# Rotary queries turned in PSUM by transposed tables and spread per head by one matmul

## The chip, the cores and the metric

The kernel runs on one core of a Trainium2 chip. The metric is the device time of one launch in microseconds. The core's engines are TensorE (PE in the profile, its weight loads PEld), VectorE (DVE), ScalarE (ACT), GpSimd (POOL) and SyncE (SP), which issues the DMAs. Each engine works through its own queue in order and waits on semaphores.

## The reference

A decoder trunk of two layers over 1024 tokens of width 1024, in f32. Each layer feeds four causal mixers in parallel, gates and merges them, and ends in a layer norm. The change lies in the first mixer (MLA), in the queries' rotary part:

```python
q = (_rms_norm(c_q, q_norm) @ w_qb).reshape(b, s, MLA_HEADS, MLA_NOPE + MLA_ROPE)   # 4 heads, 64 + 32
q_nope, q_pe = q[..., :MLA_NOPE], q[..., MLA_NOPE:]
q_pe = _rope(q_pe, cos[:, :, None, :], sin[:, :, None, :])
...
def _rope(x, cos, sin):
    x1, x2 = jnp.split(x, 2, axis=-1)
    return jnp.concatenate([x1 * cos - x2 * sin, x1 * sin + x2 * cos], axis=-1)
```

`cos` and `sin` depend on the token's position and on 16 frequencies only; they are the same for all heads and both layers. The scores are `concat(q_nope, q_pe) . concat(k_nope, k_pe)`, scaled by 96 ** -0.5.

## The kernel before

**Precision.** An f32 product is made of three fast matmuls (fp32r): each operand is split into a high part and a rest (`wh`, `wl`; `cqh`, `cql`), and high x high, low x high and high x low are added in PSUM. These are the three lines of `passes` (L255 to L257). For attention operands a helper, `stack_pair`, takes a PSUM tile with two heads of 64 channels on 128 partitions and makes two tiles, `opA` for the first head and `opB` for the second: ACT writes the rounded 64 rows (`lead`), DVE the remainder in the other 64 partitions (`rest`). In its default order it runs lead a, rest a, lead b, rest b; with `copies_first` both leads run first.

**PSUM.** There are eight banks in three pools: four for projections (`PJ`; pj, pb, pg, qpeT and so on take them in turn), two for transposes (`PT`; pt, vtp, qpe, rqb, qpT) and two for the attention output (`PY`). A tile takes a bank when the last reader of the tile before has finished.

**Order.** The program is written with generators: `run(units, filler, total)` walks the attention units and, in the gaps between their matmuls, steps a filler (the next branch's projections) so that `total` steps are spread evenly. Around the MLA queries, `main` is such a chain, and between its steps the merge of another branch is stepped (`mg`: rows pb, the branch product, pg, the merge gate, ACT's sigmoid mg and DVE's acc). The final order on each engine follows from it and from the waits.

**The stage of the MLA queries,** once per layer. `load_wq` splits three tiles of `w_qb` on POOL. `split_cq(half)` scales and splits the compressed queries of 512 tokens (row norm spread by the transposes rqb, L993). `mla_q` makes the 64 plain channels of the four heads by two pj groups of nine matmuls. `mla_qpe` makes the 4 x 32 rotary channels: nine matmuls into qpeT (channels on partitions), an ACT copy (L1028), four transposes to tokens on partitions (L1032), six DVE steps of rope (L721 to L726), a scaling on POOL (L1038), and ACT and DVE make the high part and the rest side by side (L1044, L1045), each twice over. `mla_qpT` turns these back per head, four transposes each (L1053), and ACT casts the result to `qpe` (L1055): 128 partitions that hold high, rest, high, rest of 32 channels, which the score matmul (L386) multiplies with the key's rotary part. Half 1 comes before half 0, and `mla_qpT(1)` and part of `(0)` run beside the first attention unit.

**The forgetting stage** (fox) of layer 0 is the first attention of the kernel: two runs of eight units, the first with the projections of the second pair as its filler. The values are transposed there too (vtp), and p by PT tiles (pt). `cosT` and `sinT` (128 tokens x 8 blocks x 16 frequencies) are computed by then.

Of the kernel before, what the change touches and what calls it, by code (L numbers as in the profile page):

```python
# [66 lines left out]
def decoder_trunk(ctx: ExitStack, tc: tile.TileContext, x, x_t, mem_t, positions, w_a, w_s, mla_q_norm, mla_w_qb,  # L67
# [19 lines left out]
    def nm(s):  # L87
        uid[0] += 1
        return f"{s}_{uid[0]}"
# [107 lines left out]
    c_d = dp.tile([4, S], F32, name="c_d")  # L197

# [448 lines left out]

    for layer in range(DEPTH):
# [229 lines left out]
        run(fox_units(fox[0], 0), pair_qkv(fox[1], SC64), 49)  # L878
# [126 lines left out]
        def load_wq():  # L1005
            for k in range(3):
                raw = rp.tile([P, HALF], F32, tag="wr", name=nm("wr"))
                nc.sync.dma_start(raw[:, :384], mla_w_qb[layer, k * P:(k + 1) * P, :])
                h, l = U("wqh"), U("wql")
                sv = raw[:, :384].rearrange("p (h c) -> p h c", h=4)  # L1010
                for c0, c1, d0 in ((0, 64, 0), (64, 96, 256)):
                    n = 4 * (c1 - c0)
                    hv, lv = (t[:, d0:d0 + n].rearrange("p (h c) -> p h c", h=4) for t in (h, l))
                    split_pool(sv[:, :, c0:c1], hv, lv)
                wq_h.append(h)
                wq_l.append(l)
# [6 lines left out]

        def mla_qpe(half):
            ps = PJ("qpeT")
            yield from passes(ps, wsl(wq_h, wq_l, 3, 256), cqT[half], 3)
            qT = U("qT", F32)
            act.copy(qT, ps)  # L1028
            yield QPE_STEPS
            ps = PT("qpe")  # L1030
            for b in range(4):
                pe.transpose(ps[:, b * P:(b + 1) * P], qT[:, b * P:(b + 1) * P], ident)  # L1032
            src = ps.rearrange("p (b h c) -> p b h c", b=4, h=4)
            qr = U("qr", F32).rearrange("p (b h c) -> p b h c", b=4, h=4)
            qt = TMP("qt")[:, :256].rearrange("p (b h c) -> p b h c", b=4, h=4)
            cs, sn = (t[:, 4 * half:4 * half + 4].unsqueeze(2).broadcast_to((P, 4, 4, 16)) for t in (cosT, sinT))
            rope(qr, src, cs, sn, qt, dve.tensor_tensor)
            pool.tensor_scalar(qr, qr, SC96, 1.0, ALU.mult, ALU.mult)  # L1038
            for b2 in range(2):
                t4 = wp.tile([P, 2, 4, 4, ROPE], F32R, tag="W", name=nm("qt4"))  # L1040
                for b in range(2):
                    t = t4[:, b]
                    qb_ = qr[:, 2 * b2 + b].unsqueeze(2).broadcast_to((P, 4, 2, ROPE))
                    act.copy(t[:, :, 0::2, :], qb_)  # L1044
                    dve.tensor_tensor(t[:, :, 1::2, :], qb_, f(t[:, :, 0::2, :]), ALU.subtract)  # L1045
                    t4s[half].append(t)
            yield

        def mla_qpT(half):
            for h in range(4):  # L1050
                pt = PT("qpT")
                for b in range(4):
                    pe.transpose(pt[:, b * P:(b + 1) * P].bitcast(F32R), t4s[half][b][:, h].rearrange("p a c -> p (a c)"), ident_r)  # L1053
                o = U("qpe")
                act.copy(o, pt)  # L1055
                qpe[h][half] = o
                yield
            t4s[half].clear()
# [89 lines left out]
        def step(f):  # L1148
# [3 lines left out]
        main = chain(mla_ckvT(), mla_k(0), mla_k(1), step(load_wq), step(lambda: load_cq(1)), mla_v(0), mla_v(1),  # L1152
                     split_cq(1), step(lambda: load_cq(0)), mla_qpe(1), split_cq(0), mla_q(1), mla_qpe(0), mla_qpT(1), mla_q(0), mla_qpT(0))
# [172 lines left out]
```

## Time and profile before

| | |
|---|---|
| time, median of 3 runs | 1568.74 us (1568.33 to 1569.33) |
| time of the profiled execution | 1568.4 us |
| its span on the core | 1566.7 us |
| PE busy | 1551.5 us, 99% |
| DVE busy | 1032.2 us, 66% |
| ACT busy | 724.0 us, 46% |
| POOL busy | 778.3 us, 50% |
| mean granted TensorE clock | 0.999 |

Busy rows of PE overlap one another, since a matmul starts before the one ahead has drained; the distance between two starts tells what one costs. In the groups of instructions the columns are: line, engine, operation, output and inputs, partitions x elements, count, then busy time, mean duration in ns, and the idle time in front with what ended it. In the timeline they are: start, length, engine, line, operation. In the windows: the stretch, its length, busy time of PE, PEld, DVE, ACT and POOL with the number of instructions, the granted clock, the DMA share and the GB/s.

### The profile page before, as it was taken

The page shows a single profiled execution, that of the slowest core. Times are in us where ns is not written, and L with a number is a line of the kernel's source. Part 1 is how long each engine was busy: PE and PEld are TensorE (multiplying, and loading weights), DVE is VectorE, ACT ScalarE, POOL GpSimd, SP SyncE. Part 2 cuts the span into 40 slices and gives each one's busy share as a digit, 9 for nine tenths or more (in the row PEclk, how much of TensorE's full clock was granted, in tenths as well). Part 3 has the DMA queues.
Part 4 walks back from the last instruction along what each step waited for, and adds up shares of the span by engine and source line. Part 5 has one row for each costly group of instructions (what it writes and reads, how often), then busy time and mean ns, then how long its engine had stood idle before and what let it go on. Part 6 is the DMA issues. An engine that isn't in the chain of part 4 may idle for free.

```text
span 1566.7 us, 24759 instructions
## 1 busy us (share of the span) xinstructions
PE 1551.5 (99%) x8446; PEld 1326.5 (85%) x8446; DVE 1032.2 (66%) x2055; ACT 724.0 (46%) x1608; POOL 778.3 (50%) x951
## 2 busy tenths in 40 slices
PE   9999999999999999999999999999999999999997
PEld 8888888888888888888898888888888888888886
DVE  7455687755436788872853566887554367888738
ACT  5355565545434656440323556655354346564300
POOL 5666536555544334671336655365565443346600
PEclk9999999999999999999999999999999999999999
DMA  6421112132233221252313211121322332212413
GB/s 186 115 71 42 46 47 71 58 95 82 74 110 109 73 65 31 81 175 74 125 62 101 58 51 45 41 75 51 108 70 80 103 112 73 63 37 83 154 53 115
DMA packets 86062, 127.92 MB, mean 82 GB/s; under 512 B 13425, under 2 KB 38833, under 8 KB 85937
## 3 DMA queue, kind: packets, MB, share of 16 engines
q1 hardware_dynamic: 85936, 126.34, 26.5%
q8 instruction: 67, 1.10, 0.3%
q14 instruction: 59, 0.48, 0.1%
HBM read 89.57 MB, written 19.96 MB: 70 GB/s over the span
## 4 chain that ended last, share of the span: by engine, by line
PE 97%; DVE 1%; ACT 1%; DMA 0%; issue 0%; SPq 0%; POOL 0%; DVEq 0%; ACTq 0%
PE pj L255 13%; PE pj L257 13%; PE pj L256 13%; PE y L502 8%; PE pt L472 7%; PE pb L255 4%; PE pb L256 4%; PE pb L257 4%; PE po L257 4%; PE po L256 4%; PE po L255 4%; PE sc L384 4%; PE sc L383 4%; PE pg L255 2%; PE pg L256 2%; PE pg L257 2%
## 5 line engine op out<-in xcount | busy, mean ns | idle before, releaser
L255 PE MATMUL pj<-xTh,wh 128*128 128x512 f32 x832 | 334.4, 402 | 2.3 <-DVE mx L441 1.4
L257 PE MATMUL pj<-xTh,wl 128*128 128x512 f32 x832 | 327.4, 394 | 0.0
L256 PE MATMUL pj<-xTl,wh 128*128 128x512 f32 x832 | 326.3, 392 | 0.0
L167 POOL TENSOR_TENSOR wl<-wr,wh 128x512 fp32r<-128x512 f32 x168 | 224.2, 1336 | 10.1
L156 DVE TENSOR_TENSOR pl<-pt,ph 128x384 fp32r<-128x384 f32 (+1 forms) x272 | 171.3, 638 | 84.9 <-ACT ph L155 82.8
L164 POOL TENSOR_SCALAR wh<-wr 128x512 fp32r<-128x512 f32 x168 | 113.0, 673 | 216.7 <-PE pj L256 145.6
L155 ACT CAST ph<-pt 128x384 fp32r<-128x384 f32 (+1 forms) x272 | 147.6, 549 | 156.1 <-PE pt L472 151.3
L257 PEld LDWEIGHTS pj<-xTh,wl 128*128 128x128 f32 x832 | 156.3, 188 | 31.5
L453 POOL TENSOR_SCALAR p<-p,sm 128x896 f32<-128x896 f32 (+7 forms) x128 | 101.1, 792 | 158.6 <-DVE sm L452 153.6
L255 PEld LDWEIGHTS pj<-xTh,wh 128*128 128x128 f32 x832 | 156.7, 188 | 25.1 <-DVE mx L441 1.8
L256 PEld LDWEIGHTS pj<-xTl,wh 128*128 128x128 f32 x832 | 156.7, 188 | 22.6
L135 ACT ACTIVATE p<-p,mx 128x896 f32<-128x896 f32 (+7 forms) x128 | 99.5, 777 | 72.7 <-DVE mx L441 63.6
L502 PE MATMUL y<-pl,v 128*128 128x256 f32 (+1 forms) x544 | 122.3, 302 | 0.0
L135 ACT ACTIVATE mg<-pg 128x512 f32<-128x512 f32 x128 | 76.0, 597 | 80.5 <-PE pg L257 38.6
L472 PE MATMUL pt<-ident_r,p 128*128 128x128 f32 x704 | 111.2, 273 | 0.2
L502 PE MATMUL y<-ph,v 128*128 128x256 f32 (+1 forms) x544 | 111.1, 280 | 0.0
L446 DVE TENSOR_TENSOR_SCAN kt<-kt,unseen 128x896 f32<-128x896 f32 (+3 forms) x64 | 96.0, 1502 | 20.2 <-ACT kt L135 19.7
L502 PEld LDWEIGHTS y<-ph,v 128*128 128x128 f32 x544 | 94.7, 189 | 13.5
L255 PE MATMUL pb<-ybh,wh 128*128 128x512 f32 x256 | 103.0, 402 | 0.4
L256 PE MATMUL pb<-ybl,wh 128*128 128x512 f32 x256 | 100.2, 391 | 0.0
L257 PE MATMUL pb<-ybh,wl 128*128 128x512 f32 x256 | 100.0, 391 | 0.0
L472 PEld LDWEIGHTS pt<-ident_r,p 128*128 128x128 f32 x704 | 85.7, 140 | 15.1 <-issue 0.5
(272 smaller groups left out, 3551.1 us busy)
## 6 DMA issues: line engine op xcount, KB each, us to landing
wr<-in_w_s_dram SPq DMA_DIRECT2D x168, 256.0 KB, 2.7
s<-opA SPq DMA_DIRECT2D x128, 64.0 KB, 2.0
s<-opB SPq DMA_DIRECT2D x128, 64.0 KB, 2.0
wr<-in_w_out_dram SPq DMA_DIRECT2D x32, 256.0 KB, 2.6
xr<-in_x_t_dram SPq DMA_DIRECT2D x16, 256.0 KB, 4.8
ckb<-c_d SPq DMA_DIRECT2D x8, 512.0 KB, 4.0
y_d<-y SPq DMA_DIRECT2D x16, 256.0 KB, 2.1
y<-y_d SPq DMA_DIRECT2D x16, 256.0 KB, 3.9
```

The source lines that it names most:

```text
L135: i = act.activation(*args, **kw)
L155: act.copy(h, src)
L156: return dve.tensor_tensor(l, src, f(h), ALU.subtract)
L164: i = pool.tensor_scalar(h, src, 1.0, 1.0, ALU.mult, ALU.mult)
L167: pool.tensor_tensor(l, src, f(h), ALU.subtract)
L255: pe.matmul(ps, ah, bh, start=k == 0, stop=False)
L256: pe.matmul(ps, ah, bl, start=False, stop=False)
L257: pe.matmul(ps, al, bh, start=False, stop=k == nk - 1)
L446: dve.tensor_tensor_scan(kt[:, ::-1], kt[:, ::-1], unseen[:, S - w:][:, ::-1], 1.0, ALU.mult, ALU.max)
L453: pool.tensor_scalar(p, p, sm, 1.0, ALU.mult, ALU.mult)
L472: pe.transpose(pt[:, c:c + P], self.p[i][:, b * P:(b + 1) * P], ident)
L502: pe.matmul(u.y[:, q0 * P:256], u.op["v"][b][:, u.head, :], src[:, s * 256 + q0 * P:s * 256 + 256], start=j == 0 and n == 0, stop=j == n_c ...
```

## The change

The rotation is done where the projection has left its result, in PSUM with channels on partitions. For that the tables must lie with channels on partitions too: `rotary_tables`, a generator stepped once in layer 0 behind the filler of the first fox run (`total` 53 in place of 49), spreads cosine and sine over the heads on POOL (`rows`), transposes them by blocks (`tab`), scales them on ACT (the sine with its sign per 32 rows) and stores them (`tab_d`). Each layer loads them by halves. In `mla_qpe` four DVE multiplications of 32 partitions take the swapped halves times sine from PSUM, one multiplies the PSUM tile by cosine in place, one adds in place. For this the weight columns are laid out so that the 128 channels are, for each of two pairs of heads, first half of both, second half of both. `stack_pair` then makes two stacked tiles, and in `mla_qpT` one matmul per head with a selection matrix (`pick`, copied from the identity) spreads them to the layout that `qpe` had.

```diff
+    def rotary_tables():
+        for n, src in enumerate((cosT, sinT)):
+            for half in range(2):
+                rows = U("rows", F32)
+                pool.tensor_scalar(rows.rearrange("p (b r c) -> p b r c", b=4, r=8),
+                                   src[:, 4 * half:4 * half + 4, :].unsqueeze(2).broadcast_to((P, 4, 8, 16)), 1.0, 1.0, ALU.mult, ALU.mult)
+                ps = PT("tab")
+                for b in range(4):
+                    pe.transpose(ps[:, b * P:(b + 1) * P], rows[:, b * P:(b + 1) * P], ident)
+                t = TMP("tab")
+                if n == 0:
+                    act.activation(t, ps, AF.Copy, scale=SC96)
+                else:
+                    for r0 in range(0, P, 32):
+                        act.activation(t[r0:r0 + 32, :], ps[r0:r0 + 32, :], AF.Copy, scale=-SC96 if r0 % 64 else SC96)
+                nc.sync.dma_start(tab_d[half][:, n, :], t)
+                yield
...
-        run(fox_units(fox[0], 0), pair_qkv(fox[1], SC64), 49)
+        tables = () if layer else rotary_tables()
+        run(fox_units(fox[0], 0), chain(pair_qkv(fox[1], SC64), tables), 49 if layer else 53)
...
+        def load_tabs(half):
+            tabs[half] = K("tab").rearrange("p (a n) -> p a n", a=2)
+            nc.sync.dma_start(tabs[half], tab_d[half])
+            if not pick:
+                pick.append(U("pick")[:, :2 * P].rearrange("p (e r q c) -> p e r q c", e=2, r=2, q=4))
+                for e in range(2):
+                    for r in range(2):
+                        act.copy(pick[0][:, e, r], ident.rearrange("p (q e c) -> p e q c", q=4, e=2)[:, e])
+
         def mla_qpe(half):
             ps = PJ("qpeT")
             yield from passes(ps, wsl(wq_h, wq_l, 3, 256), cqT[half], 3)
-            qT = U("qT", F32)
-            act.copy(qT, ps)
+            tab = tabs.pop(half)
+            t = U("qt", F32)
+            for r0 in range(0, P, 32):
+                r1 = r0 + 32 if r0 % 64 == 0 else r0 - 32
+                dve.tensor_tensor(t[r0:r0 + 32, :], ps[r1:r1 + 32, :], tab[r1:r1 + 32, 1], ALU.mult)
+            dve.tensor_tensor(ps, ps, tab[:, 0], ALU.mult)
+            dve.tensor_tensor(ps, ps, t, ALU.add)
             yield QPE_STEPS
-            ps = PT("qpe")
...
+            d = [[None, None], [None, None]]
+            stack_pair(d, 1.0)(ps, half)
+            t4s[half] += [d[0][half], d[1][half]]
             yield
 
         def mla_qpT(half):
             for h in range(4):
                 pt = PT("qpT")
-                for b in range(4):
-                    pe.transpose(pt[:, b * P:(b + 1) * P].bitcast(F32R), t4s[half][b][:, h].rearrange("p a c -> p (a c)"), ident_r)
+                pe.matmul(pt, pick[0][:, h % 2].rearrange("p r q c -> p (r q c)"), t4s[half][h // 2], start=True, stop=True)
```

In `main`, `load_tabs(1)` follows `load_cq(1)` and `load_tabs(0)` follows `load_cq(0)`. In `load_wq` the rotary columns of a weight tile are split in two pieces of 64 columns (one per pair of heads) where one piece of 128 stood.

Three places show how the order moves. First TensorE behind the last matmuls of half 1's qpeT in layer 0. Before, a pb and a pg group are followed by the transposes of qpe and rqb and then by the first pj group of `mla_q(1)`:

```order
L255 MATMUL pb_5990<-ybh_5394,wh_5749 128x512
L256 MATMUL pb_5990<-ybl_5395,wh_5749 128x512
L257 MATMUL pb_5990<-ybh_5394,wl_5750 128x512
L255 MATMUL pg_6009<-mrh_3836,wh_5749 128x512
L256 MATMUL pg_6009<-mrl_3837,wh_5749 128x512
L257 MATMUL pg_6009<-mrh_3836,wl_5750 128x512
L1032 MATMUL qpe_5925<-ident_r,qT_5902 128x128 x4
L993 MATMUL rqb_5949<-ident_r,rq_643 128x128 x4
L255 MATMUL pj_5999<-cqh_5836,wqh_5643 128x512
```

After, between the two pj groups of `mla_q(1)` on the same engine (the first ends here, the second begins), a pg group and the first two spreading matmuls:

```order
L256 MATMUL pj_6048<-cqh_5927,wqh_5710 128x512
L257 MATMUL pj_6048<-cql_5928,wqh_5710 128x512
L258 MATMUL pj_6048<-cqh_5927,wql_5711 128x512
L256 MATMUL pg_6111<-mrh_3790,wh_5806 128x512
L257 MATMUL pg_6111<-mrl_3791,wh_5806 128x512
L258 MATMUL pg_6111<-mrh_3790,wl_5807 128x512
L1081 MATMUL qpT_6154<-opA_5992,pick_5732 128x512
L1081 MATMUL qpT_6158<-opA_5992,pick_5732 128x512
L256 MATMUL pj_6070<-cqh_5896,wqh_5690 128x512
```

The transposes of qpe are gone, and both groups of rqb stand together far ahead; the first qpeT_5945 has 24 matmuls from its own last to this pj_6070, which takes its bank, and pj_6048 takes the bank of pb_5977. Second, DVE at the same place. Before, the rotation (qr, qt), the row norm of the compressed queries (cq) and acc alternate:

```order
L721 TENSOR_TENSOR qr_5930<-qpe_5925,cosT 128x16x16
L722 TENSOR_TENSOR qt_5931<-qpe_5925,sinT 128x256
L724 TENSOR_TENSOR qr_5930<-qpe_5925,sinT 128x16x16
L995 TENSOR_TENSOR cq_5877<-cq_5877,rqb_5949 128x512
L995 TENSOR_TENSOR cq_5879<-cq_5879,rqb_5949 128x512
L995 TENSOR_TENSOR cq_5881<-cq_5881,rqb_5949 128x512
L723 TENSOR_TENSOR qr_5930<-qr_5930,qt_5931 128x16x16
```

After:

```order
L1017 TENSOR_TENSOR cq_5941<-cq_5941,rqb_5998 128x512
L1069 TENSOR_TENSOR qt_5964<-qpeT_5945,tab_5730 32x512 x4
L1133 SCALAR_TENSOR_TENSOR acc_5984<-mg_5975,pb_5977 128x512
L1070 TENSOR_TENSOR qpeT_5945<-qpeT_5945,tab_5730 128x512
L1071 TENSOR_TENSOR qpeT_5945<-qpeT_5945,qt_5964 128x512
L313 SCALAR_TENSOR_TENSOR opA_5992<-qpeT_5945,opA_5992 64x512
L313 SCALAR_TENSOR_TENSOR opB_5993<-qpeT_5945,opB_5993 64x512
```

The quarter multiplications now stand ahead of the acc that reads pb_5977, and all of the rotation and stacking reads the PSUM tile qpeT_5945. Third, TensorE in layer 0's first fox run, where after the change the cosine's two tab groups stand around a score pair ahead of a projection group:

```order
L258 MATMUL pj_1681<-xTh_212,wl_1422 128x512
L659 MATMUL tab_1603<-ident_r,rows_1601 128x128 x4
L384 MATMUL sc_1798<-opA_1295,opA_1041 128x256
L385 MATMUL sc_1798<-opA_1295,s_349_1652 128x256
L659 MATMUL tab_1613<-ident_r,rows_1611 128x128 x4
L256 MATMUL pj_1807<-xTh_397,wh_1415 128x512
```

Before, the projection groups run on between the same kind of rows (s is the query with its halves swapped, loaded by SP):

```order
L257 MATMUL pj_1634<-xTh_203,wl_1455 128x512
L383 MATMUL sc_1734<-opA_1321,opA_1049 128x128
L384 MATMUL sc_1734<-opA_1321,s_337_1605 128x128
L255 MATMUL pj_1634<-xTh_211,wh_1454 128x512
L256 MATMUL pj_1634<-xTl_212,wh_1454 128x512
```

The sine's two groups follow 20 rows later, side by side, and the next transposes of p (pt) some 30 rows behind them.

More of the change, by code (lines that the diff above doesn't have):

```diff
@@ L197, in decoder_trunk @@
     c_d = dp.tile([4, S], F32, name="c_d")
+    tab_d = dp.tile([2, P, 2, HALF], F32, name="tab_d")
     def rsqrt(dst, m, n):
@@ L1010, in load_wq @@
                 sv = raw[:, :384].rearrange("p (h c) -> p h c", h=4)
[L1011 to L1014, printed above, removed]
+                hv, lv = (t[:, :256].rearrange("p (h c) -> p h c", h=4) for t in (h, l))
+                split_pool(sv[:, :, 0:64], hv, lv)
+                for g in range(2):
+                    d0 = 256 + 64 * g
+                    hv, lv = (t[:, d0:d0 + 64].rearrange("p (t e c) -> p t e c", t=2, e=2) for t in (h, l))
+                    split_pool(sv[:, 2 * g:2 * g + 2, 64:96].rearrange("p e (t c) -> p t e c", t=2), hv, lv)
                 wq_h.append(h)
@@ L1022, in mla_q @@
                 stack_pair(ml[pair]["q"], SC96, True)(ps, half)
+        tabs = {}
+        pick = []
+        def load_tabs(half):
[6 more added lines that the diff above has]
+                        act.copy(pick[0][:, e, r], ident.rearrange("p (q e c) -> p e q c", q=4, e=2)[:, e])
         def mla_qpe(half):
@@ L1026, in mla_qpe @@
             yield from passes(ps, wsl(wq_h, wq_l, 3, 256), cqT[half], 3)
-            qT = U("qT", F32)
-            act.copy(qT, ps)
-            yield QPE_STEPS
-            ps = PT("qpe")
-            for b in range(4):
[L1032 to L1046, printed above, removed]
+            tab = tabs.pop(half)
[5 more added lines that the diff above has]
+            dve.tensor_tensor(ps, ps, t, ALU.add)
+            yield QPE_STEPS
+            d = [[None, None], [None, None]]
+            stack_pair(d, 1.0)(ps, half)
+            t4s[half] += [d[0][half], d[1][half]]
             yield
@@ L1051, in mla_qpT @@
                 pt = PT("qpT")
-                for b in range(4):
-                    pe.transpose(pt[:, b * P:(b + 1) * P].bitcast(F32R), t4s[half][b][:, h].rearrange("p a c -> p (a c)"), ident_r)
+                pe.matmul(pt, pick[0][:, h % 2].rearrange("p r q c -> p (r q c)"), t4s[half][h // 2], start=True, stop=True)
                 o = U("qpe")
@@ L1150, in step @@
             yield
-        main = chain(mla_ckvT(), mla_k(0), mla_k(1), step(load_wq), step(lambda: load_cq(1)), mla_v(0), mla_v(1),
-                     split_cq(1), step(lambda: load_cq(0)), mla_qpe(1), split_cq(0), mla_q(1), mla_qpe(0), mla_qpT(1), mla_q(0), mla_qpT(0))
+        main = chain(mla_ckvT(), mla_k(0), mla_k(1), step(load_wq), step(lambda: load_cq(1)), step(lambda: load_tabs(1)), mla_v(0), mla_v(1),
+                     split_cq(1), step(lambda: load_cq(0)), step(lambda: load_tabs(0)), mla_qpe(1), split_cq(0), mla_q(1), mla_qpe(0), mla_qpT(1), mla_q(0), mla_qpT(0))
         def early():
```

## The prediction

> **What bounds the kernel.** I read the page from the top (busy time, then the chain that ended last), then the windows around the two places that the change touches, then the timeline there.
>
> ```profile
> span 1566.7 us, 24759 instructions
> ...
> PE 1551.5 (99%) x8446; PEld 1326.5 (85%) x8446; DVE 1032.2 (66%) x2055; ACT 724.0 (46%) x1608; POOL 778.3 (50%) x951
> ...
> PE 97%; DVE 1%; ACT 1%; DMA 0%; issue 0%; SPq 0%; POOL 0%; DVEq 0%; ACTq 0%
> ```
>
> TensorE is the path: 97% of the chain. Work taken from another engine is worth something only where TensorE waits for it, and a new wait of TensorE costs its full length.
>
> ```profile
> 75.00:160.00 85.00, 84.19 (x475) 72.20 (x475) 51.53 (x145) 46.14 (x102) 54.55 (x82) 1.00 0.22 60
> 485.00:532.00 47.00, 46.13 (x236) 37.90 (x235) 32.41 (x72) 26.23 (x53) 12.73 (x14) 1.00 0.21 60
> 1265.00:1312.00 47.00, 46.15 (x237) 37.92 (x236) 32.35 (x72) 26.17 (x53) 12.75 (x14) 1.00 0.20 60
> ```
>
> The first column after the length is PE, then PEld, DVE, ACT and POOL. The first window lies in layer 0's forgetting-attention stage, where the tables will be built; the others are the MLA query stage of the two layers. All are full on PE, and the two layers are alike, so I cost one MLA stage and double it. The clock is 1.00.
>
> A busy TensorE row overlaps the next, so I price matmuls by the distance between starts:
>
> ```profile
> 495.09 0.39 PE L256 MATMUL qpeT<-cql,wqh 128*128 128x512 f32 x1
> 495.31 0.39 PE L257 MATMUL qpeT<-cqh,wql 128*128 128x512 f32 x1
> ...
> 500.31 0.60 PE L1032 MATMUL qpe<-ident_r,qT 128*128 128x128 f32 x4
> 500.75 0.60 PE L993 MATMUL rqb<-ident_r,rq 128*128 128x128 f32 x4
> 501.10 0.48 PE L255 MATMUL pj<-cqh,wqh 128*128 128x512 f32 x1
> 501.42 0.39 PE L256 MATMUL pj<-cql,wqh 128*128 128x512 f32 x1
> ...
> 505.07 0.39 PE L257 MATMUL pj<-cqh,wql 128*128 128x512 f32 x1
> 505.56 0.47 PE L255 MATMUL qpeT<-cqh,wqh 128*128 128x512 f32 x1
> ...
> 513.85 0.60 PE L1032 MATMUL qpe<-ident_r,qT 128*128 128x128 f32 x4
> 514.20 0.30 PE L1053 MATMUL qpT<-ident_r,qt 128*128 128x128 f32 x1
> 514.34 0.45 PE L255 MATMUL pj<-cqh,wqh 128*128 128x512 f32 x1
> 514.62 0.39 PE L256 MATMUL pj<-cql,wqh 128*128 128x512 f32 x1
> ...
> 519.96 0.40 PE L257 MATMUL pj<-cqh,wql 128*128 128x512 f32 x1
> 520.20 0.79 PE L1053 MATMUL qpT<-ident_r,qt 128*128 128x128 f32 x8
> 520.82 0.47 PE L383 MATMUL sc<-opA,opA 128*128 128x512 f32 x1
> 521.13 0.40 PE L384 MATMUL sc<-opA,s 128*128 128x512 f32 x1
> ...
> 524.72 0.40 PE L257 MATMUL pg<-mrh,wl 128*128 128x512 f32 x1
> 525.68 0.53 PE L1053 MATMUL qpT<-ident_r,qt 128*128 128x128 f32 x4 [0.57 <-ACT qpe L1055]
> ...
> 527.67 0.50 PE L255 MATMUL pb<-ybh,wh 128*128 128x512 f32 x1
> ```
>
> A 512-column matmul takes 0.227 us (495.09 to 495.31; 505.07 would have been followed at 505.30). Four f32 transposes take 0.35 (500.75 to 501.10, 0.088 each), a short one 0.078 (8 from 520.20 to 520.82). The matmul behind a group of transposes starts its follower about 0.08 late (501.10 to 501.42 is 0.32), which I call the switch.
>
> **What goes on TensorE, per layer.** The two groups at L1032 go: 0.44 (500.31 to 500.75) and 0.35 (513.85 to 514.20), and one switch of 0.09, as the two rqb groups now stand side by side: -0.88. Head 0's four transposes, which lie singly between pj matmuls from 514.20 on, go: 4 x 0.078 and three switches of 0.06 (514.34 to 514.62 is 0.28): -0.49. The two spreading matmuls that take their place outside the start of attention: 2 x 0.227 = +0.45. The gap of 0.26 at 505.07 ends when qpeT of half 0 finds its operands; it now comes a pair of pj groups later, so it goes: -0.26.
>
> The start of attention, 519.96 to 527.67, holds the other 28 transposes. By count they cost 28 x 0.078 and five switches, 2.58; six matmuls cost 1.36, so 1.2 us could go. But this stretch waits: for ACT's casts of qpT (0.57 at 525.68) and for DVE's row maxima, and the casts stay, eight of them, behind the same leads of the new query tiles. Walking the new order with these durations, the same wait for a cast grows from 0.7 to 1.0 and the stretch ends at 7.0 to 7.2 us in place of 7.71: -0.6, half of the count.
>
> **What comes, per layer: a bank held by a chain.** Before, one ACT copy (L1028) freed the qpeT bank. Now DVE multiplies it by quarters, multiplies and adds it in place, and the stacking helper takes it in four steps, ACT and DVE in turn:
>
> ```profile
> L1105 DVE SCALAR_TENSOR_TENSOR acc<-mg,pb 128x512 f32<-128x512 f32 x32 | 21.9, 684 | 9.2 <-PE pb L257 7.4 <-POOL wl L167 1.7
> L1109 DVE TENSOR_TENSOR pb<-pb,acc 128x512 f32<-128x512 f32 x32 | 22.2, 693 | 0.4
> L312 DVE SCALAR_TENSOR_TENSOR opA<-pj,opA 64x512 fp32r<-64x512 f32 x56 | 38.3, 684 | 44.8 <-ACT opA L308 22.7 <-ACT opB L308 12.3 <-PE pj L257 5.5
> ...
> 49.01 0.59 ACT L308 ACTIVATE opA<-pj 64x512 fp32r<-64x512 f32 x1 [4.00 <-PE pj L257]
> 50.35 0.59 ACT L308 ACTIVATE opB<-pj 64x512 fp32r<-64x512 f32 x1 [0.75 <-DVE opA L312]
> ...
> 50.98 0.69 DVE L312 SCALAR_TENSOR_TENSOR opB<-pj,opB 64x512 fp32r<-64x512 f32 x1 [0.66 <-ACT opB L308]
> ...
> 500.95 0.42 DVE L721 TENSOR_TENSOR qr<-qpe,cosT 128x256 f32<-128x256 f32 x1 [6.16 <-PE qpe L1032]
> 501.29 0.41 DVE L722 TENSOR_TENSOR qt<-qpe,sinT 128x256 f32<-128x256 f32 x1
> ...
> 501.95 1.87 DVE L995 TENSOR_TENSOR cq<-cq,rqb 128x512 f32<-128x512 f32 x3
> ```
>
> The trace has no row of 32 partitions. Its 64x512 rows take 684 ns and the 128x512 rows 684 to 693, so partitions do not shorten an operation and columns do (128x256: 414 to 424). I take a 32x512 quarter as one of the 128x512 rows that run back to back at 0.62 (three in 1.87). The lower end is the 128x256 row at 0.34 (500.95 to 501.29), the upper 0.72, a 0.69 row with nothing overlapped.
>
> For half 1, count from the start of the last qpeT matmul. Data and start-up 0.48; four quarters 4 x 0.62 = 2.48, end 2.96; then DVE's order has an acc, 0.62, end 3.58; the in-place multiply and add, each waiting for the one before, 2 x 0.66, end 4.9; the stacking steps 49.01 to 51.67 (50.98 + 0.69), 2.66, and with the handovers the bank is free at 7.66. TensorE has 24 matmuls to run until the pj that takes this bank: the last qpeT, nine of pb and pg, nine of the first pj, three pg, two spreading ones: 24 x 0.227 = 5.45. It loses 7.66 - 5.45 = +2.21. It loses it in two places: 1.4 at the first pj, whose bank is the one that the acc behind the four quarters reads (free at 3.65, wanted at 2.27), and 0.8 at the second. With quarters at 0.34 the loss is 1.1, at 0.72 it is 2.6. Queued behind the waiting pj are only TensorE's own matmuls; ACT's casts of half 0's queries stand behind its leads and are wanted 4 us later.
>
> For half 0 the chain takes about 8.3 (two acc steps lie in it), and 39 matmuls, 8.9 to 9.1, run before a score matmul needs the bank: no stall, with 0.7 to spare. Were that cover gone, it would cost what the chain exceeds it by.
>
> Sum per layer: -0.88 - 0.49 + 0.45 - 0.26 - 0.6 + 2.21 = +0.43, so +0.9 for two.
>
> **The tables, once.** Sixteen f32 transposes in four groups: 16 x 0.088 + 4 x 0.09 = +1.77 on a TensorE that has 0.8 us of slack in the 85 of that window. Around them:
>
> ```profile
> L164 POOL TENSOR_SCALAR wh<-wr 128x512 fp32r<-128x512 f32 x168 | 113.0, 673 | 216.7 <-PE pj L256 145.6
> ...
> L308 ACT ACTIVATE opA<-pj 64x512 fp32r<-64x512 f32 x56 | 33.0, 589 | 45.5 <-PE pj L257 41.7 <-DMA ckb<-c_d 3.4
> ```
>
> POOL makes four rows (4 x 0.67 = 2.7, before the softmax scalings and weight splits queued behind them). ACT copies two tables of 128x512 (2 x 0.59) and eight 32-row pieces; by the 64x512 row, as on DVE, 0.59 each, 4.7 in all. Behind these in ACT's queue stand a softmax exponential, the leads of the next pair and the y copies. TensorE has the projection of the next pair to run meanwhile, some 60 matmuls until the next p transposes need the same two PSUM banks, so I cost the waits at +0.1, from 0 to 2.4 (a sine group's four copies, uncovered). Stage: +1.9.
>
> The rest I cost at nothing. SP's four stores and the 0.5 MB of table loads per half come hundreds of microseconds before their use (ahead of the memory rows in SP's queue; the DMA share is 0.20 to 0.22 in the windows). POOL's six extra split pieces per layer and ACT's four small pick copies lie in a stretch where POOL is busy 12.7 of 47 us and ACT 26; POOL's scalings, ACT's qT copies and DVE's old rotation were themselves covered, so taking them away gives nothing.
>
> Total +0.9 + 1.9 = +2.8 on the profiled 1568.4; the median of the runs is 1568.74, and 0.2%, about 3.1 us, is what a measurement can tell from no change. I predict 1571.3, under that limit (1571.9) by little.
>
> On the matmul's price the Trainium skill, "TensorE: Matmul & The Clock Gate", section "Back-to-back issue gap", gives a sustained 81 ns for 128 columns and 131 ns for 512. The first agrees with the 78 to 88 ns here; for the second these f32-stored matmuls show 227, so the trace decides. By the page the 16 spreading matmuls would cost 1.5 us less, an estimate, and the total would be +1.3.
>
> **Rivals.**
> *The quarters are short* (columns and partitions both count, near 0.34). For it: nothing in the trace is as small as 32x512, and the 256-column rows show that fixed cost is only 0.1 to 0.2. Against: 64 partitions saved nothing. The loss falls to 1.1 per layer: +2.8 - 2.2 = +0.6, 1569.1.
> *The chain is covered*, because the bank does not stand in the way of the two pj groups, and the start of attention gives its full count. Against: each of the two pj groups must wait for the last reader of its bank, and such waits exist already, as this row of the waits shows (total, count, longest):
>
> ```profile
> PE pj L255 <- DVE opB L312: 0.9, 2, 0.5
> ```
>
> No stall gives +2.8 - 4.4 = -1.6; the full 1.2 and the casts' 0.57 besides give another -2.3 for two layers: 1564.8, faster.
> *The table pass holds TensorE* (the other side). Four groups go through the two banks in which values and p are transposed, and the last two are emptied by four copies each, one after the other, in a queue with softmax work; the y copies behind them take the sine tiles' two buffers and so wait for stores that stand in SP's queue behind a weight load. For it: no step of that stage is free on TensorE, 84.19 of 85. Uncovered, each sine group costs 2.4 less the work between, and the y copies behind them hold TensorE's next y: +2.4 to +4, 1573.7 to 1575.5. It decides from 0.6 us of wait on.
>
> **How the numbers follow.** My sum 0.50 (own range 1570.0 to 1572.6; about a quarter of that above 1571.9), short quarters 0.15, a covered chain 0.12 (of which 0.08 beyond the limit), the table pass 0.23. Faster by over 0.2% 0.09, within 0.55, slower 0.36. The range runs from the better half of the covered case to the costly tables: 1566.0 to 1575.0.
>
> **What would show it.** After the change, TensorE should have a wait of about 1.4 us before the first pj group behind qpeT of half 1 (released by DVE acc) and of 0.8 before the second (by DVE opB), in both layers; a 32x512 DVE row of 0.6 to 0.69; half 0 without a wait; and 519.96 to 527.67's stretch shorter by 0.6. In layer 0's forgetting stage 16 tab transposes and no wait over 0.3. I am wrong if the quarters last under 0.5, if pj takes its bank without waiting, or if y or pt waits for ACT in layer 0's forgetting stage.

## The result, and the profile after

| | before | after |
|---|---|---|
| median of 7 runs | 1569.33 us (1568.33 to 1569.68) | 1574.25 us (1572.48 to 1574.45) |
| profiled execution, its span | 1568.4, 1566.7 us | 1574.45, 1572.7 us |

The ratio is 1.003, with a 95% interval of 1.0018 to 1.0042: 4.9 us slower. The forecast was 1571.3, with 1566 to 1575 as its range; the sign was the one of its sum (+2.8), the size was not. On a second chip the two kernels gave 1573.73 and 1568.43 us, a ratio of 1.0032 (1.002 to 1.0045); one of the changed kernel's six runs there was a slow one of 3978.52 us, which the ratio leaves out.

The page of the changed kernel, its lines on the span, the engines and the chain:

```profile
span 1572.7 us, 24690 instructions
...
PE 1551.3 (99%) x8398; PEld 1324.0 (84%) x8398; DVE 1039.1 (66%) x2047; ACT 729.0 (46%) x1614; POOL 778.6 (50%) x963
...
PE 94%; DVE 3%; DMA 1%; ACT 1%; issue 0%; POOL 0%; SPq 0%; DVEq 0%; ACTq 0%; POOLq 0%
```

TensorE is as busy as before (1551.3 against 1551.5 us), in a span that is 6.0 longer, and its share of the chain fell from 97% to 94%, DVE's rose from 1% to 3% (a share tells where the chain passes, and not what it costs). So on balance TensorE had as much work as before and the added time is waiting, most of it for DVE. To see where, I cut both traces at TensorE instructions that both have: the last pA matmul of layer 0 (the end of the beginning), the last v matmul of each layer's MLA part, the first pb behind the last qpT (the end of the MLA query stage), and the end.

| us | before | after | difference |
|---|---|---|---|
| beginning | 31.81 | 33.40 | +1.59 |
| forgetting stage, up to the MLA stage | 455.42 | 458.16 | +2.74 |
| MLA query stage, layer 0 | 40.44 | 41.02 | +0.58 |
| from there to layer 1's MLA stage | 739.79 | 739.79 | 0.00 |
| MLA query stage, layer 1 | 40.44 | 41.03 | +0.59 |
| from there to the last matmul | 250.31 | 250.87 | +0.56 |

The windows of the second and the third line, before and then after (the first column after the length is PE):

```profile
31.81:487.23 455.42, 454.02 (x2527) 390.01 (x2526) 276.86 (x528) 224.98 (x512) 261.33 (x334) 1.00 0.26 76
487.23:527.67 40.44, 39.58 (x200) 32.31 (x198) 27.90 (x56) 22.07 (x44) 7.38 (x8) 1.00 0.21 61
```

```profile
33.40:491.56 458.16, 456.81 (x2547) 392.11 (x2546) 273.90 (x524) 231.07 (x526) 262.42 (x344) 1.00 0.26 79
491.56:532.59 41.03, 37.56 (x165) 29.65 (x163) 31.69 (x53) 21.33 (x39) 6.41 (x7) 1.00 0.21 61
```

They read quite differently. In the forgetting stage TensorE is 2.79 us busier and idle as little as before (1.35 against 1.40): what came is plain work on the bound engine. In the MLA stage it is 2.02 us less busy, so the saving is there, but idle for 3.47 us in place of 0.86, which is 2.6 more. DVE's time there rises from 27.9 to 31.7.

The counts in these windows show one thing more. The forgetting stage (the first line of each pair) has 20 matmuls more, and only 16 are the tables'. The other four are one group of the rqb transposes. Before, one group ran ahead of the last v matmul, at which I cut, and one behind it (500.75); now both run ahead of it, side by side. Before and after:

```profile
472.49 0.60 PE L993 MATMUL rqb<-ident_r,rq 128*128 128x128 f32 x4
472.84 0.48 PE L255 MATMUL pj<-ckTh,wkvh 128*128 128x512 f32 x1
```

```profile
476.40 1.03 PE L1015 MATMUL rqb<-ident_r,rq 128*128 128x128 f32 x8
477.19 0.48 PE L256 MATMUL pj<-ckTh,wkvh 128*128 128x512 f32 x1
```

The second group lengthens the first by 0.44 us (0.79 from the first rqb to the pj, in place of 0.35). So 0.44 of the forgetting stage's +2.74 has only moved there from the MLA stage: the tables cost 2.3, and the MLA stage, like for like, got 1.02 us longer and not 0.58. The same four transposes moved ahead of layer 1's MLA stage (1.03 there), into the stretch whose difference is 0.00; what shortened that stretch by as much was not found, and it scatters by 0.4 between executions of one kernel.

TensorE's timeline in layer 0's MLA stage of the changed kernel: the last matmul of half 1's qpeT, then the two waits, then the start of attention.

```profile
502.36 0.39 PE L258 MATMUL qpeT<-cqh,wql 128*128 128x512 f32 x1
...
504.40 0.39 PE L258 MATMUL pg<-mrh,wl 128*128 128x512 f32 x1
506.35 0.50 PE L256 MATMUL pj<-cqh,wqh 128*128 128x512 f32 x1 [1.56 <-DVE acc L1133]
506.69 0.39 PE L257 MATMUL pj<-cql,wqh 128*128 128x512 f32 x1
...
509.21 0.62 PE L1081 MATMUL qpT<-opA,pick 128*128 128x512 f32 x2
510.40 0.50 PE L256 MATMUL pj<-cqh,wqh 128*128 128x512 f32 x1 [0.56 <-DVE opB L313]
510.73 0.40 PE L257 MATMUL pj<-cql,wqh 128*128 128x512 f32 x1
...
525.26 0.39 PE L258 MATMUL pj<-cqh,wql 128*128 128x512 f32 x1
...
530.45 0.50 PE L1081 MATMUL qpT<-opB,pick 128*128 128x512 f32 x1 [0.59 <-ACT qpe L1083]
...
532.59 0.47 PE L256 MATMUL pb<-ybh,wh 128*128 128x512 f32 x1 [0.44 <-DVE opB L313]
```

The row at 504.40 would have been followed at 504.63, so the first wait is 1.72 us (the bracket counts from the modelled end of the row ahead and says 1.56). The second is 510.40 less 509.66, 0.74. The matmul behind each wait starts its follower 0.1 late (506.35 to 506.69). DVE's rows of the same place are the chain that it waits for:

```profile
502.79 2.79 DVE L1069 TENSOR_TENSOR qt<-qpeT,tab 32x512 f32<-32x512 f32 x4 [3.09 <-PE qpeT L258]
505.61 0.69 DVE L1133 SCALAR_TENSOR_TENSOR acc<-mg,pb 128x512 f32<-128x512 f32 x1
506.22 0.69 DVE L1070 TENSOR_TENSOR qpeT<-qpeT,tab 128x512 f32<-128x512 f32 x1
506.95 0.70 DVE L1071 TENSOR_TENSOR qpeT<-qpeT,qt 128x512 f32<-128x512 f32 x1
508.31 0.68 DVE L313 SCALAR_TENSOR_TENSOR opA<-qpeT,opA 64x512 fp32r<-64x512 f32 x1 [0.66 <-ACT opA L309]
509.65 0.69 DVE L313 SCALAR_TENSOR_TENSOR opB<-qpeT,opB 64x512 fp32r<-64x512 f32 x1 [0.66 <-ACT opB L309]
```

The four quarters take 2.79, 0.70 each; the acc that frees the first pj's bank ends at 506.30; the last rest ends at 510.34 and the second pj starts at 510.40.

### The profile page after: what moved, and what is told of

The parts are those of the page before. It is cut to its first block, busy times and chain, and to the rows that moved or that the text cites. A ratio compares the mean times of both kernels' runs of the same rounds, so it can differ in the third digit from the quotient of the medians.

```text
span 1572.7 us, 24690 instructions
## 1 busy us (share of the span) xinstructions
PE 1551.3 (99%) x8398; PEld 1324.0 (84%) x8398; DVE 1039.1 (66%) x2047; ACT 729.0 (46%) x1614; POOL 778.6 (50%) x963
## 4 chain that ended last, share of the span: by engine, by line
PE 94%; DVE 3%; DMA 1%; ACT 1%; issue 0%; POOL 0%; SPq 0%; DVEq 0%; ACTq 0%; POOLq 0%
PE pj L256 13%; PE pj L258 13%; PE pj L257 13%; PE y L503 8%; PE pt L473 7%; PE po L256 4%; PE po L257 4%; PE po L258 4%; PE pb L256 4%; PE sc L385 4%; PE sc L384 4%; PE pb L257 3%; PE pb L258 3%; PE pg L256 2%; PE pg L257 2%; PE pg L258 2%
```

## The experiments

Theory: the change costs the forgetting stage the tables' matmul time, and in each MLA stage the chain that holds the qpeT bank eats what the transposes gave back. The stages of every run, cut as above (MLA stages of layer 0; those of layer 1 differ by at most 0.04, in e2 by 0.3). The ratios are to runs of the kernel before on the same chip; there were three chips, with 1568.57 us for it beside e1 to e4, 1568.65 beside e5 to e8 and 1568.43 beside the rest. The second rqb group lies in the forgetting stage in every run but e4 and c11. In layer 1 two pg matmuls (0.23 us each) more lie in the MLA stage in e8 and e9, three in e2 and e5.

| run | median us | ratio to before (95%) | forgetting stage | MLA stage |
|---|---|---|---|---|
| e1, late and in SBUF | 1570.29 | 1.001 (1.0001 to 1.0019) | 458.20 | 39.69 |
| e2, late only | 1575.29 | 1.0047 (1.0035 to 1.006) | 458.21 | 43.25 |
| e3, no tables | 1570.02 | 1.001 (1.0002 to 1.0019) | 455.86 | 41.03 |
| e4, tables only | 1571.28 | 1.0017 (1.0008 to 1.0026) | 457.70 | 40.40 |
| e5, half 1 late | 1567.90 | 0.9995 (0.9987 to 1.0004) | 458.17 | 39.13 |
| e6, spread first | 1565.85 | 0.9982 (0.9973 to 0.9991) | 458.17 | 38.58 |
| e7, cheap tables | 1563.72 | 0.9967 (0.9954 to 0.9979) | 455.41 | 38.58 |
| e8, two products | 1569.57 | 1.0006 (0.9997 to 1.0014) | 458.23 | 39.62 |
| e9, SBUF only | 1570.98 | 1.0016 (1.0007 to 1.0024) | 458.17 | 40.15 |
| c10, the change again | 1573.73 | 1.0032 (1.002 to 1.0045) | 458.17 | 41.02 |
| c11, before again | 1569.19 (one run) | | 455.41 | 40.44 |

These two stages repeat to 0.03 us between executions of one kernel, so they resolve differences that the medians hide. The two other stretches move more: the one between the MLA stages took 739.79 and 739.41 us in two executions of the changed kernel, the last one 250.87 and 251.11; over all runs they lie between 738.25 and 740.47, and between 249.23 and 251.63.

**e1, e2, e9: what holds the banks.** e1 makes two edits at `mla_qpe`; e2 has the first alone (the two moved yields), e9 the second (the tile `c`).

```diff
             yield from passes(ps, wsl(wq_h, wq_l, 3, 256), cqT[half], 3)
+            yield QPE_STEPS
...
-            dve.tensor_tensor(ps, ps, tab[:, 0], ALU.mult)
-            dve.tensor_tensor(ps, ps, t, ALU.add)
-            yield QPE_STEPS
+            c = U("qc", F32)
+            dve.tensor_tensor(c, ps, tab[:, 0], ALU.mult)
+            dve.tensor_tensor(c, c, t, ALU.add)
+            yield
...
-            stack_pair(d, 1.0)(ps, half)
+            stack_pair(d, 1.0)(c, half)
```

> The changed kernel with three edits of one kind in the MLA stage: the multiplications by the tables come after the three merge steps (so DVE does the acc first), the cosine product goes to an SBUF tile, and the add and the stacking read that tile; so the qpeT bank is held by five DVE operations in place of ten ACT and DVE steps. Theory (bank chain): both waits of TensorE behind qpeT of half 1, 1.72 and 0.74 us in each layer, vanish, since TensorE needs the banks 5.0 us after the last qpeT matmul and they are free at 4.0 and before: 4.9 us less than the changed kernel, about 1569.3 and equal to the kernel before within 1 us. Rival (the time goes to the longer DVE work itself, and what waits would wait for it elsewhere): the waits move to the spreading matmuls or to the first scores and the time stays above 1572.5.

The time, 1570.29, is 1 us above what was expected and clear of the rival's 1572.5. The two waits behind qpeT are gone from e1's trace, and the MLA stage fell from 41.02 to 39.69, by 1.33 and not by 2.46: part came back at the start of attention. These rows of e1 show it: DVE idle before half 0's products, TensorE waiting for a cast, and, at half 1, both leads of the stacking following at once.

```profile
516.71 0.69 DVE L1135 SCALAR_TENSOR_TENSOR acc<-mg,pb 128x512 f32<-128x512 f32 x1 [1.18 <-PE pb L258]
517.43 2.79 DVE L1070 TENSOR_TENSOR qt<-qpeT,tab 32x512 f32<-32x512 f32 x4
...
523.65 0.50 PE L1083 MATMUL qpT<-opB,pick 128*128 128x512 f32 x1 [1.13 <-ACT qpe L1085]
```

```profile
506.16 0.63 ACT L309 ACTIVATE opA<-qc 64x512 fp32r<-64x512 f32 x1 [4.11 <-DVE qc L1073]
506.82 0.63 ACT L309 ACTIVATE opB<-qc 64x512 fp32r<-64x512 f32 x1
...
506.83 0.69 DVE L313 SCALAR_TENSOR_TENSOR opA<-qc,opA 64x512 fp32r<-64x512 f32 x1
507.54 0.69 DVE L313 SCALAR_TENSOR_TENSOR opB<-qc,opB 64x512 fp32r<-64x512 f32 x1
```

From 506.16 to 508.23 the stacking takes 2.07 us from SBUF; from PSUM it took 2.66 in the changed kernel (507.68 to 510.34, the second lead waiting for the first rest).

> Only the first of those edits: the multiplications and the add, still in place in PSUM, come after the merge steps, so that DVE's acc stands ahead of them. Theory (bank chain): the wait for acc (1.72 us) vanishes, but the spreading matmul then waits for the first rest (6.0 us after the last qpeT matmul, wanted at 5.0) and the second pj a little for an acc: about 1.25 us of waits per layer in place of 2.46, 2.4 us less than the changed kernel, about 1571.9. Rival (the place in DVE's order does nothing, only the length of the chain counts): the same 2.46 us per layer, 1574.3.

A miss: the stage got 2.2 us longer. Behind half 1 it went about as expected: the wait for acc is gone, and one wait for the first rest is left (0.93 us by its bracket). But half 0's products, now behind two acc steps too, began 2.45 us later in the stage than in the changed kernel (520.08, where the stage starts at 491.79; 517.40 and 491.56 there), its leads with them, and behind these in ACT's queue a cast for which TensorE waited 2.27 us. Then TensorE ran slow:

```profile
526.96 0.50 PE L1082 MATMUL qpT<-opB,pick 128*128 128x512 f32 x1 [2.27 <-ACT qpe L1084]
...
528.30 0.63 PE L1082 MATMUL qpT<-opB,pick 128*128 128x512 f32 x1
528.73 0.63 PE L1082 MATMUL qpT<-opA,pick 128*128 128x512 f32 x1
```

```profile
524.00:527.00 3.00, 0.73 (x5) 0.27 (x3) 1.69 (x3) 1.86 (x4) 0.00 (x0) 1.00 0.00 0
527.00:530.00 3.00, 3.00 (x8) 2.06 (x9) 1.32 (x4) 2.01 (x4) 0.00 (x0) 0.60 0.00 0
```

The windows' third column from the right is the granted clock: 0.60 for the 3 us behind a stretch in which TensorE was busy for 0.73 of 3.00. In the window 527.62 to 531.03 it is 0.50, and so it is for 3.41 us in layer 1. A 512-column matmul then takes 0.43 (528.30 to 528.73) in place of 0.227. Neither theory had that; it is told again below. It is also not in every execution: the profiled one (1578.49 us) and one more (1577.63) have a mean granted clock of 0.996, the other three (1573.92 to 1575.29) have 0.998 or 0.999. So the 43.25 us hold for an execution with the lower clock; the other three are about as slow as the changed kernel, and still not the 2.4 us faster that was expected.

> Of e1's edits only the second: the cosine product goes to an SBUF tile, and the add and the stacking read that tile; the multiplications stay where the change put them in DVE's queue. Theory (bank chain): TensorE needs a bank 2.3 us after the last qpeT matmul that is free after five DVE operations at 4.0, so one wait of about 1.75 us is left per layer in place of 2.46, and the four stacking steps take 2.0 in place of 2.7 us, since ACT and DVE no longer take turns at one PSUM bank: the MLA stage, 41.0 us in the changed kernel and 40.4 before, comes to 39.7 to 40.2, about 1572 in all. Rival (the order alone decides, e1 owes everything to it): 41.0 as in the changed kernel.

Near what the theory said: one wait is left in each layer, for the cosine product, 2.6 us for the two by this row of the waits (total, count, longest), and the stage is 40.15, at the upper end of what was expected.

```profile
PE pj L256 <- DVE qc L1071: 2.6, 2, 1.5
```

So of the 1.33 us that e1 gained per layer the tile in SBUF gives 0.87, and the order adds 0.46 only together with it. The rival, that the order alone decides, is out.

**e8: four products or two.**

```diff
-            for r0 in range(0, P, 32):
-                r1 = r0 + 32 if r0 % 64 == 0 else r0 - 32
-                dve.tensor_tensor(t[r0:r0 + 32, :], ps[r1:r1 + 32, :], tab[r1:r1 + 32, 1], ALU.mult)
+            for r0 in (0, 64):
+                r1 = 64 - r0
+                dve.tensor_tensor(t[r0:r0 + 64, :], ps[r1:r1 + 64, :], tab[r1:r1 + 64, 1], ALU.mult)
```

> The changed kernel, but the four sine products of 32 partitions become two of 64 (the halves of the tile are swapped in place of the halves of each pair, so the rotation is a wrong one). Theory (a DVE operation costs by its columns, whatever its partitions): 1.4 us less in each half's chain; behind half 1 the two waits of TensorE shrink from 2.46 to about 1.1 us per layer: 2.8 us less than the changed kernel, about 1571.5. Rival (64 partitions take twice 32): no change, 1574.3.

```profile
L1069 DVE TENSOR_TENSOR qt<-qpeT,tab 64x512 f32<-64x512 f32 x8 | 5.5, 687 | 5.9 <-PE qpeT L258 5.8
```

64 partitions take 687 ns, as 32 do (688 in the changed kernel). Layer 0's MLA stage fell by 1.40 us, the length of the two operations left out, so the chain's length passes to TensorE one for one. The median fell by more, 4.7 against the changed kernel's 1574.25 on another chip, where the two MLA stages account for 2.8 (3.3 with the two pg matmuls that came into layer 1's); the rest was not traced.

**e3, e4: the tables by themselves.**

```diff
     def rotary_tables():
-        for n, src in enumerate((cosT, sinT)):
-            for half in range(2):
-                rows = U("rows", F32)
...
+        t = TMP("tab")
+        pool.memset(t, SC96)
+        for n in range(2):
+            for half in range(2):
+                nc.sync.dma_start(tab_d[half][:, n, :], t)
+        yield
```

> The changed kernel without the making of the tables: one POOL memset and four stores of a constant stand in place of POOL's spreading, 16 transposes, ten ACT copies; the rotation then uses wrong factors, everything else is as in the changed kernel. Theory: 2.7 us go in layer 0's forgetting stage, of which 1.8 are the transposes and 0.9 waits, and nothing elsewhere: about 1571.5. Rival (the tables are hidden and all the loss is in the MLA stage): 1574.3.

e4 is the kernel before with `tab_d`, the full `rotary_tables` and its place in the first fox run, and nothing else:

```diff
-        run(fox_units(fox[0], 0), pair_qkv(fox[1], SC64), 49)
+        tables = () if layer else rotary_tables()
+        run(fox_units(fox[0], 0), chain(pair_qkv(fox[1], SC64), tables), 49 if layer else 53)
```

> The kernel before with the making and storing of the tables added as in the change, and nothing that reads them. Theory: 1.8 to 2.7 us more than the kernel before, 1571 to 1572. Rival (the tables cost only where later work has moved too): within 0.5 us of the kernel before.

Taken out, the tables give 2.30 us of the forgetting stage back (458.16 to 455.86); put in alone, they cost 2.28 (455.42 to 457.70), and the MLA stage stays as it was in either (41.03, 40.40). The two halves of the change add up and do not meet. In e3 TensorE's busy time in that stage is 454.48 of 455.86, in the changed kernel 456.81 of 458.16: work, and no wait, where the expectation had put 0.9 of waits. The 0.44 by which e3's forgetting stage exceeds the 455.42 before is the rqb group. (The total of the filler's steps, 53 with the tables, is 50 in e3, as three fewer are left to make.)

**e5, e6, e7: a version that keeps the saving.** e5 is e1 with half 0's products at once; e6 is e5 with half 1's spreading ahead (the last pair of lines below, cut to the order that matters); e7 is e6 with another making of the tables.

```diff
-            yield QPE_STEPS
+            if half:
+                yield QPE_STEPS
             tab = tabs.pop(half)
...
-            yield
+            yield 0 if half else QPE_STEPS
...
-                     ... mla_q(1), mla_qpe(0), mla_qpT(1), mla_q(0), mla_qpT(0))
+                     ... mla_q(1), mla_qpT(1), mla_qpe(0), mla_q(0), mla_qpT(0))
```

> As e1 (products in SBUF), but only half 1 waits for the merge steps before it multiplies; half 0 multiplies at once. In e1 both waits behind qpeT of half 1 were gone, yet 1.4 to 2 us per layer came back at the start of attention, where half 0's chain ended late because its multiplications stood behind two acc steps (DVE idle 1.18 us before them). Theory (place of half 0 in DVE's queue): half 0's chain ends about 1.4 us earlier per layer, 2.8 us less than e1: about 1567.5. Rival (DVE is full in this stage, so its order cannot matter): as e1, 1570.3.

> As e5, and half 1's four spreading matmuls and casts are put ahead of half 0's rotation in the program, so that ACT makes them while it is idle and not behind half 0's leads. Theory (ACT's queue holds the casts back at the start of attention): the first wait for a cast there, 1.1 us in e1, goes, and two of the later ones shrink: 1.0 to 1.5 us per layer less than e5, about 1565. Rival (TensorE waits there for DVE's row maxima anyway): as e5.

e5 came to 1567.90 and e6 to 1565.85, near what was expected (1567.5 and 1565), and both rivals fell by the medians. Layer 0's MLA stage gained less than expected, 0.56 and 0.55 us in place of 1.4 and of 1.0 to 1.5. In layer 1 e5 gained 1.2, since its stage holds the three pg matmuls besides; in e6 these are ahead of it again, and the stage is 38.58 as in layer 0. So the medians came near the forecast partly by what lies outside these stages: e5's last stretch (249.91) is 1.5 us shorter than e1's (251.40), of which layer 1's wait of a pb for DVE, told below and not in e5's trace, is 0.8; e6's (249.29) is 0.6 shorter again. This is not explained. In e6 TensorE's busy time in the stage is 37.6 of 38.58.

```diff
     def rotary_tables():
         for n, src in enumerate((cosT, sinT)):
-            for half in range(2):
-                rows = U("rows", F32)
...
+            t = TMP("tab")
+            dve.transpose(t[:, :P], src.rearrange("p b c -> p (b c)"))
+            for q in range(4):
+                for e in range(2):
+                    r = 32 * q + 16 * e
+                    nc.sync.dma_start(tab_s[n].rearrange("c (g e q i) -> c g e q i", g=4, e=2, q=4)[:, :, e, q, :],
+                                      t[r:r + 16, :P].rearrange("c (g i) -> c g i", g=4))
+            yield
+        for half in range(2):
+            for n in range(2):
+                nc.sync.dma_start(tab_d[half].rearrange("(a c) n s -> a c n s", a=8)[:, :, n],
+                                  tab_s[n, :, half * HALF:(half + 1) * HALF].unsqueeze(0).broadcast_to((8, 16, HALF)))
+        yield
...
-                dve.tensor_tensor(t[r0:r0 + 32, :], ps[r1:r1 + 32, :], tab[r1:r1 + 32, 1], ALU.mult)
-            dve.tensor_tensor(c, ps, tab[:, 0], ALU.mult)
+                dve.scalar_tensor_tensor(t[r0:r0 + 32, :], ps[r1:r1 + 32, :], -SC96 if r1 % 64 else SC96, tab[r1:r1 + 32, 1], ALU.mult, ALU.mult)
+            dve.scalar_tensor_tensor(c, ps, SC96, tab[:, 0], ALU.mult, ALU.mult)
```

> As e6, and the tables are turned by two DVE block transposes of 32x32 in place of POOL's spreading, TensorE's 16 transposes and ACT's ten copies; the head replication is left to DMAs in DRAM, scale and sign to the multiplications. Theory (the tables cost what they put on TensorE): the 2.7 us of the forgetting stage go: e6 less 2.7, about 1562.5, faster than the kernel before by 0.4%. Rival (twenty more DMAs in SP's queue delay the swapped queries and weights there): e6 or slower.

```profile
32.34:487.75 455.41, 454.17 (x2532) 390.32 (x2530) 276.55 (x530) 225.51 (x516) 262.82 (x340) 1.00 0.27 80
487.75:526.33 38.58, 37.63 (x164) 29.75 (x163) 31.87 (x53) 22.12 (x40) 6.39 (x7) 1.00 0.22 65
```

```profile
109.86 0.31 DVE L653 STREAM_TRANSPOSE tab<-cosT 128x128 f32<-128x128 f32 x1
114.01 0.30 DVE L653 STREAM_TRANSPOSE tab<-sinT 128x128 f32<-128x128 f32 x1
```

The forgetting stage is back at the 455.4 us of the kernel before, with the rqb group in it: two DVE operations of 0.3 us, and DMAs, stand where the change put 2.3 us on TensorE, and other matmuls of the stage got 0.4 shorter (told below). At 1563.72 us, a ratio of 0.9967 (0.9954 to 0.9979), e7 beats the kernel before by 0.3% and the change by 0.6%. Of the 4.9 us to the kernel before, the MLA stages give 3.7; in its trace the last stretch is 1.1 shorter (249.23) and the one between the MLA stages 0.6 (739.24), for reasons that were not sought.

**c10, c11: both kernels again.** Nothing is edited in either.

> The changed kernel again, against the kernel before on this chip. Theory (the change costs 2.7 in the forgetting stage and 0.6 in each MLA stage; the 1.6 us that the profiled run lost in the first 33 us and 0.6 in the last stage are spread between executions): 3.9 us over the kernel before, with a beginning shorter than 33.4 us. Rival (the beginning is slower in the changed program): 5 to 6 us over the kernel before, and 33.4 again.

> The kernel before again, for its stages. Theory: forgetting stage to MLA stage 455.4 us and each MLA stage 40.4 us as in the first profile, and a beginning anywhere from 31.8 to 33.5 us (31.81 in the first profile). Rival (the beginning belongs to the program): 31.8 again.

The forgetting and MLA stages came back to 0.03 us. The beginnings did not: 31.94 for the changed kernel (33.40 in the first profile), 32.42 for the one before (31.81); those of all the other runs lie between 31.8 and 33.6, without relation to the edit. Where the beginning was longest (33.40, and 33.59 in e2), five DVE rows at about 20 us took 7.19 us. In the profile before, in the one after, and in c10 they are:

```profile
20.33 5.45 DVE L156 TENSOR_TENSOR xTl<-xr,xTh 128x512 fp32r<-128x512 f32 x5
```

```profile
20.85 7.19 DVE L156 TENSOR_TENSOR xTl<-xr,xTh 128x512 fp32r<-128x512 f32 x5
```

```profile
20.46 5.02 DVE L156 TENSOR_TENSOR xTl<-xr,xTh 128x512 fp32r<-128x512 f32 x5
```

These rows are not the whole of it (5.02 us in c11 too, with a beginning of 32.42). As the changed kernel began with 31.94 us in c10, the 1.59 us of the beginning are not shown to be the change's. Its median in c10, however, was 5.3 us over the kernel before, where the forgetting and MLA stages account for 3.9 and the last stretch for 0.6 to 0.8; about a microsecond between the medians stays unexplained.

## Why the prediction was right or wrong

- **The number.** 1574.25 lies 2.9 us above the forecast, and outside the sum's own range of 1570.0 to 1572.6. It is inside the whole range only because that was stretched to 1575.0 for the rival in which the table pass holds TensorE, and that rival's waits did not come. So that the range holds is luck. The larger chance (0.55) had gone to a result within 0.2%, 0.36 to a slower one. (The sum by itself gives 1571.2 on the profiled time and 1571.5 on the median.)
- **The bound and the two places** were right: TensorE, the forgetting stage of layer 0, and half 1 of each MLA stage. Of the five differences in the table of stages, three lie there; the other two are the beginning and the last stretch.
- **The MLA stage** was forecast at +0.43 per layer, with both rqb groups counted in it. Like for like it took 1.02 more. The terms that were too small are the next three, 0.25, 0.2 and 0.2; TensorE's own savings came out within 0.1 of the forecast.
- **The chain that holds the bank** is the part whose mechanism held best: waits of 1.4 and 0.8 forecast, 1.72 and 0.74 measured, on the releasers named (acc, opB), in both layers. The sum of 2.21 became 2.46, mainly because the quarter was sized at 0.62, from rows that overlap, and takes 0.70 (2.79 for four); 0.72 was the upper end. The price goes by columns and not by partitions (32 partitions 688 ns, 64 in e8 687), so the rival of short quarters is out; the two waits put the rival of a covered chain out too.
- **The two slow starts** behind these waits, 0.1 each, were missing from the sum.
- **The start of attention** took 7.33 us (525.26 to 532.59) where 7.0 to 7.2 were forecast, so it gave 0.4 and not 0.6.
- **Half 0** has no wait, as forecast, but the margin was thinner: the bank is free at 525.40 (DVE's last rest at 524.71), the score matmul starts at 525.72. In e1 and e2 half 0's chain ended later, and TensorE then waited for something else that hangs on it: ACT's casts, which stand behind half 0's leads.
- **The tables** were forecast at +1.9 and took 2.3. There was no wait: TensorE's rows of waits around them are the same before and after, so the rival in which the table pass holds TensorE by ACT's copies or the stores is out too. From the end of the beginning to the first rqb, the distances between TensorE's starts add up to 2.32 us more than before. The 16 tab transposes are 1.50 of it and the pj matmuls, as many as before, 0.41; together that is the forecast's size. The rest, 0.4, is spread over p's transposes (0.23) and the score matmuls (0.19), whose numbers are also as before, and I had put it at nothing. Four more filler steps cut the groups there at other places, which would do this. In e7, with three more steps and no tables on TensorE, the same sum is 0.41 less than before, most of it in the same kinds of rows, and in e3, with one more, it is the same to 0.03. That the cutting is the cause was not tried by itself.
- **The last stretch** (+0.56) was not in the prediction. In layer 1's last merge a pb waits for DVE's mg:

```profile
PE pb L256 <- DVE mg L1143: 0.5, 1, 0.5
```

The wait is also in the traces of e1 and e2 (0.8 us each), e8 (0.2) and c10 (0.3), and in none of e3, e4, e5, e6, e7 and e9, so it hangs on how the steps of the merge fall; why was not settled. It is not all: c10's last stretch is longer (251.11) with a shorter wait.
- For a 512-column matmul, the 131 ns of the Trainium skill, "TensorE: Matmul & The Clock Gate", section "Back-to-back issue gap", were rightly set aside. The two spreading matmuls of e9 that run without a wait take 0.23 each (start at 509.85, the next row at 510.31).

## What to carry to other kernels

When work is taken off the bound engine by giving another engine a longer chain on the same PSUM tile, count how many matmuls lie between the tile's last write and the next use of its bank, and let the chain leave PSUM by its first operations; here five DVE operations in place of ten steps, and their place in the queue, were worth 1.33 us in each MLA stage, and 2.44 with half 0's products at once and the spreading ahead. Work that is needed once belongs on an engine with room: the same tables cost 2.3 us as TensorE transposes and nothing that shows as DVE block transposes with DMAs. And compare stages beside the medians: cut at common instructions, the two stages that the change touches repeat to 0.03 us, where the medians of the kernel before differ by 0.9 from one set of runs to another. But count the instructions on both sides of the cut, since a group that slips across it looks like a cost on one side and a saving on the other.

## What the runs showed of the hardware that I had not expected

- In the profiled execution of e2, TensorE's granted clock fell to 0.50 for 3.41 us in both layers, from 527.62 and from 1309.27 on, with matmuls at 0.43 us in place of 0.227. In layer 0 a stretch of 3 us came before in which TensorE was busy for 0.73, with a wait of 2.27 us in it; in layer 1 the longest such wait is 2.3 too. Waits of 1.7 us in the changed kernel did not lower it (1.00). The Trainium skill, "TensorE: Matmul & The Clock Gate", section "What's actually happening", puts the threshold at an idle window of about 3.4 us. Here the fall came behind a shorter wait. By the mean clocks it came in two of e2's five executions only, and what decides was not tried.
- ACT and DVE take turns on a PSUM tile (2.66 us for the four stacking steps) and overlap on an SBUF tile (2.07), with single operations no shorter (ACT 0.63 from SBUF and 0.59 from PSUM, DVE 0.69 and 0.68 to 0.69). These waits end on the other engine's instruction, so what shows is the program's ordering of the two engines; that the chip itself would hold them apart was not tried.
- A DVE block transpose of 128x128 f32 takes 0.30 to 0.31 us. The Trainium skill, "VectorE: DVE Perf Modes", section "The three transpose paths", gives 311 ns for bf16.
